# Token forms over all quarters of their stage, S5 parameters in short pieces and S5 two steps later, in a hybrid retention and S5 decoder step on Trainium2

## The chip, the core and the metric

The kernel runs on one core of one Trainium2 chip. The core has five engines that run their own instruction streams and meet at semaphores: TensorE (PE: matmuls, and PEld for its weight loads), VectorE (DVE), ScalarE (ACT), GpSimd (POOL) and SyncE (SP). Transfers are issued by an engine (here SP, ACT and POOL) and carried by 16 DMA engines. The metric is the time of one execution on the device, in microseconds (us); less is better.

## The reference

One step of a decoder layer over 1024 prompt tokens and 8 sample tokens (1032 columns in all), model width 2048, all in fp32. It is cut here to what matters:

```python
h = rmsnorm(x, g_pre)
proj = h @ w_in                                   # 2048 x 10240
q, k, v, za, ub, zb, ga, gb = split(proj)         # 1024 each, ga and gb 2048
ya = retention(rope(q), rope(k), v, s_ret)        # 8 heads, chunks of 128
yb = s5(ub, ...)                                  # 64 groups, 64 complex states each
ya = (ya * silu(za)) @ w_pa
yb = (yb * silu(zb)) @ w_pb
out = (sigmoid(ga) * ya + sigmoid(gb) * yb) @ w_out
return x + rmsnorm(out, g_post), the new states
```

and the parameters of S5, which the kernel computes from the weights before S5 can begin:

```python
dt = exp(log_dt); mag = exp(lam_re * dt)
abar_r, abar_i = mag * cos(lam_im * dt), mag * sin(lam_im * dt)
coef = (abar - 1) / lam                           # complex
bbar = coef * b                                   # and powers of abar for chunks of 128
```

## The kernel before

Every matmul is done in fp32 by a split: a weight quarter (128 x 512) comes on SP's queue, ACT makes its rounded copy `whi` (L193), DVE the remainder `wlo` (helper `tt`, L84), and PE multiplies `whi` with the high and the low part of the activations and `wlo` with the high part (`three`, L200 to L202). PE runs through the program with almost no gaps. All else is fitted beside it by hand: `bg` is a queue of generators, and `slot()` (L164) runs the next piece of the first of them, up to its next `yield`. The instructions of a piece are placed behind those that PE, ACT and DVE have just been given. So the number of pieces and the number of slots decide when a generator ends; `drain()` runs what is left of all of them at once.

The stages that the change touches, in the order of the program:

1. **Start.** The tokens are loaded and split, two of the eight S5 input tiles (`ubp`, pool `ubw`, two buffers) are computed, and the token norm `rstd`. `scale_ub` scales these two tiles by it on DVE.
2. **Forms stage** (L758 to L760). `linear` computes the other S5 inputs, `M_UB + 3` to `M_UB + 7`: four weight quarters each, 36 matmuls a quarter, and a slot after each, so 20 slots. After the fourth quarter `evac_ub` empties the three PSUM banks of the tile into a `ubp` buffer on DVE (five instructions) and POOL writes the buffer to DRAM (`ub_d`). In the slots `build_forms` (L737) runs: eight rounds, each of which loads two rows of 128 features over all tokens (tile `fx`, four buffers, POOL's queue), scales them on DVE (L744), makes four differences and sums (tiles `fo`, five buffers), and writes seven forms `fm_d` on ACT's queue (L751). These are the activations of a Strassen scheme with seven products.
3. **Product loop** (L1209). 70 steps: 35 pairs of output tiles, for the first half of the features (steps 0 to 34) and for the second. A step has seven products of 24 matmuls (`product`, L857), each with its weights made two products ahead (`prep`, `whi` at L838), and a slot behind each. The results of a product leave PSUM on ACT or DVE (`evac_st`: tiles `p`, `u`, `st`); product 3 writes the bank that product 1 used, and so on, so a late `u` on DVE stops PE. POOL writes four results per step to DRAM (`pt_d`).
4. In step 1 the generator `s5_params` (L379) is put into `bg`: small vector work on tiles of 128 x 64 to 128 x 256. Before, it has six pieces. In step 3 what is left of it is drained, its pool is released, and `s5_all` follows, which has one piece for each of 200 slots, and `s5_out` with one more. S5 uses PE, DVE, ACT and POOL between the products.
5. In step 34 (`NP - 1`) S5's pools are released and the pool `stg2` with twelve buffers takes their place. Through it the 28 token forms of the second half are read back (`stage`, L800, POOL's queue) and split (`unstage`: cast on ACT at L245, difference on DVE at L84) into the activation tiles, form by form as the products of step 34 free them. Step 35 begins the second half.

The order of the instructions on each engine is that of the program as a scheduler lays it out: a load of `stg2` can stand ahead of the results of an earlier step.

Of the kernel before, what the change touches and what calls it, by code (L numbers as in the profile page):

```python
# [10 lines left out]
F32 = mybir.dt.float32  # L11
# [10 lines left out]
TOK = SEQ + NB  # L22
KD = D // 128
# [55 lines left out]
def emit(ctx, tc, I, O):  # L79
# [254 lines left out]
    ubw = ubstack.enter_context(tc.tile_pool(name="ubw", bufs=2))  # L334
# [44 lines left out]
    def s5_params():  # L379
# [16 lines left out]
        def fexp(out, x):  # L396
# [8 lines left out]
            V.scalar_tensor_tensor(t, n, -LN2_LO, t, ALU.mult, ALU.add)  # L405
            V.tensor_scalar(p, t, EXP_POLY[0], None, ALU.mult)
            for cc in EXP_POLY[1:] + [1.0]:
                V.scalar_tensor_tensor(p, p, cc, t, ALU.add, ALU.mult)
            V.tensor_scalar(n, n, 127.0, 8388608.0, ALU.add, ALU.mult)
# [4 lines left out]
        fexp(dt, ld)  # L414
# [3 lines left out]
        fexp(mag, lx)  # L418
        yield
# [6 lines left out]
        V.tensor_scalar(ph, ph, MAGIC, None, ALU.subtract)  # L426
        rr = pt("rr", 2 * N)
# [5 lines left out]
        V.tensor_scalar(rr, rr, PI_CLAMP, -PI_CLAMP, ALU.min, ALU.max)  # L433
        sc = pt("sc", 2 * N)
# [15 lines left out]
        V.reciprocal(den, den)  # L450
        mul(cr, nr, lrs)
# [7 lines left out]
        pp["cr"], pp["ci"] = cr, ci  # L459
        AR = s5q.tile([128, 9, S], F32, name="AR")  # L460
# [6 lines left out]
        for d in (1, 2, 4):  # L467
            s_, o_ = slice(1, d + 1), slice(d + 1, 2 * d + 1)
            br = AR[:, d:d + 1, :].broadcast_to([128, d, S])
            bi = AI[:, d:d + 1, :].broadcast_to([128, d, S])  # L470
            mul(AR[:, o_], AR[:, s_], br)
            mul(t1[:, 0:d], AI[:, s_], bi)
            sub(AR[:, o_], AR[:, o_], t1[:, 0:d])
            mul(AI[:, o_], AR[:, s_], bi)
            mul(t1[:, 0:d], AI[:, s_], br)
            add(AI[:, o_], AI[:, o_], t1[:, 0:d])
        pp["AR"], pp["AI"] = AR, AI
        yield
# [12 lines left out]
        for i in range(10):  # L491
# [12 lines left out]
            if i % 4 == 3:  # L504
                yield
# [231 lines left out]
    def build_forms():  # L737
        for i in range(KD // 8 * 4):
            kh, i = divmod(i, 4)
            t = {}  # L740
            for n, k in (("u", 8 * kh + i), ("v", 8 * kh + 4 + i)):
                r = fb.tile([128, TOK], F32, name="fx", bufs=4)
                P.dma_start(r, I["xT"][k])
                V.scalar_tensor_tensor(r, r, gpre[:, k:k + 1], rstd, ALU.mult, ALU.mult)  # L744
                t[n + "1"], t[n + "2"] = r[:, 0:HT], r[:, HT:TOK]
            for n, a, b, op in (("t1", "u1", "u2", ALU.subtract), ("t3", "u2", "v2", ALU.subtract),
# [6 lines left out]
            yield  # L753
# [455 lines left out]
    for s in range(len(steps)):  # L1209
# [7 lines left out]
        if s == 3:  # L1217
# [406 lines left out]
```

## Time and profile before

| | us |
|---|---|
| median of 3 runs | 2696.56 (2695.28 to 2698.29) |
| the profiled execution, its own time | 2691.63 |
| its span in the profile | 2689.8 |
| mean granted clock of PE in it | 0.995 |

The span runs from the first to the last recorded instruction; the profiled execution took 1.8 us more than that. In a timeline a row is: start, busy time, engine, line, operation, output and inputs with their shapes, how many instructions of one kind in a row, and in brackets how long the engine was idle ahead of them and what released it. In a window the row begins with its stretch and length, then the busy time of PE, PEld, DVE, ACT and POOL with the number of instructions, the granted clock of PE (1.00 is full speed), the busy share of the DMA engines and what they moved in GB/s. PE's wide matmuls of the product loop follow one another every 0.12 us, so 24 of them take 2.9 us, and a step of seven products 20.2 us.

### The profile page before, as it was taken

How to read it: one execution, taken by the hardware profiler on the slowest of the kernel's cores; microseconds unless marked ns; L12 is line 12 of the kernel's file. 1: busy time of each engine (PE TensorE's matmuls, PEld its weight loads, DVE VectorE, ACT ScalarE, POOL GpSimd, SP SyncE). 2: the span in 40 equal slices, each digit the busy share in tenths (PEclk: the TensorE clock that was granted, in tenths of full speed). 3: DMA queues.
4: the chain of work that ended last, by engine and by line, in shares of the span. 5: the costliest groups of instructions: out<-in, count | busy, mean ns of one | idle time of the engine just before them, and what ended most of it. 6: DMA issues, size and time to landing. Idle time of an engine off the chain costs nothing.

```text
span 2689.8 us, 50001 instructions
## 1 busy us (share of the span) xinstructions
PE 2640.3 (98%) x19268; PEld 2572.4 (96%) x19268; DVE 1706.6 (63%) x3648; ACT 906.2 (34%) x1607; POOL 743.4 (28%) x1205
## 2 busy tenths in 40 slices
PE   9999999999999999999999999999999999999988
PEld 8999999999999999999999999999999999998866
DVE  6645988988988867558867666665422344335455
ACT  6013232332333335442234444444411122333333
POOL 0103222222222222322244434332032354112020
PEclk9999999999999999999999999999999999999999
DMA  5886444444444457876688778777244444435575
GB/s 186 273 249 195 136 127 124 123 127 132 119 130 127 125 175 215 207 194 158 164 224 231 212 204 215 185 211 241 77 147 141 137 142 142 146 125 184 166 238 167
DMA packets 209615, 458.71 MB, mean 171 GB/s; under 512 B 30832, under 2 KB 51776, under 8 KB 209248
## 3 DMA queue, kind: packets, MB, share of 16 engines
q0 software_dynamic: 87344, 252.19, 33.5%
q1 hardware_dynamic: 102496, 180.63, 22.1%
q10 hardware_dynamic: 19536, 22.69, 2.8%
q8 instruction: 151, 2.47, 0.4%
q14 instruction: 88, 0.72, 0.1%
HBM read 318.12 MB, written 137.27 MB: 169 GB/s over the span
## 4 chain that ended last, share of the span: by engine, by line
PE 85%; DVE 5%; DMA 5%; issue 3%; ACT 2%; POOL 1%; ACTq 0%; DVEq 0%; SPq 0%; POOLq 0%
PE acc L857 46%; PE mm L200 9%; PE mm L201 9%; PE mm L202 9%; PE mm L1524 5%; PE misc L1524 1%; DMA wraw<-in_w_outB 1%; DVE wlo L84 1%; DVE a L84 1%; DMA fm_d<-fo 1%; DVE u L84 1%; PE misc L621 1%; PE misc L699 1%; PE misc L698 1%; PE misc L1064 1%
## 5 line engine op out<-in xcount | busy, mean ns | idle before, releaser
L857 PE MATMUL acc<-a,whi 128*128 128x258 f32 x7840 | 1276.8, 285 | 14.0 <-DVE u L84 7.8
L857 PEld LDWEIGHTS acc<-a,whi 128*128 128x128 f32 x7840 | 1079.8, 190 | 21.4 <-DVE u L84 9.8
L857 PE MATMUL acc<-a,wlo 128*128 128x258 f32 x3920 | 790.1, 283 | 0.0
L84 DVE TENSOR_TENSOR wlo<-wraw,whi 128x512 fp32r<-128x512 f32 x547 | 384.3, 703 | 417.8 <-ACT whi L193 334.9
L857 PEld LDWEIGHTS acc<-a,wlo 128*128 128x128 f32 x3920 | 607.2, 190 | 0.0
L200 PE MATMUL mm<-a,whi 128*128 128x384 f32 (+2 forms) x1584 | 513.3, 325 | 12.2 <-ACT whi L193 7.9
L201 PE MATMUL mm<-a,whi 128*128 128x384 f32 (+2 forms) x1584 | 513.1, 324 | 0.2 <-DVE a L352 0.2
L202 PE MATMUL mm<-a,wlo 128*128 128x384 f32 (+2 forms) x1584 | 511.4, 323 | 0.3
L838 ACT CAST whi<-wraw 128x512 fp32r<-128x512 f32 x280 | 173.7, 620 | 503.1 <-PE acc L857 393.4
L193 ACT CAST whi<-wraw 128x512 fp32r<-128x512 f32 x267 | 165.0, 619 | 521.7 <-PE mm L201 328.7
L200 PEld LDWEIGHTS mm<-a,whi 128*128 128x128 f32 x1584 | 298.4, 189 | 13.4 <-ACT whi L193 8.3
L202 PEld LDWEIGHTS mm<-a,wlo 128*128 128x128 f32 x1584 | 299.9, 189 | 1.6 <-DVE wlo L84 1.5
L201 PEld LDWEIGHTS mm<-a,whi 128*128 128x128 f32 x1584 | 298.7, 189 | 0.6 <-DVE a L352 0.6
L838 ACT CAST whi<-wr 128x512 fp32r<-128x512 f32 x210 | 130.1, 620 | 417.4 <-PE acc L857 390.4
L84 DVE TENSOR_TENSOR wlo<-wr,whi 128x512 fp32r<-128x512 f32 x210 | 143.7, 684 | 42.9 <-ACT whi L838 41.8
L1524 PE MATMUL mm<-whi,a 128*128 128x512 f32 x352 | 121.7, 403 | 4.0 <-ACT whi L193 4.0
L84 DVE TENSOR_TENSOR st<-mm,sz 128x384 f32<-128x384 f32 (+1 forms) x96 | 49.4, 515 | 92.8 <-PE mm L202 53.2
L84 DVE TENSOR_TENSOR wraw<-wr 128x512 f32<-128x512 f32 x140 | 95.9, 685 | 1.7
L911 POOL DMA_DIRECT2D u<-pt_d x70 | 62.0, 886 | 114.1 <-DVE u L84 92.7
L84 DVE TENSOR_TENSOR p<-acc,p 128x516 f32<-128x516 f32 x70 | 48.4, 692 | 67.1 <-PE acc L857 67.0
L909 POOL DMA_DIRECT2D pt_d<-u x70 | 38.7, 553 | 188.5 <-DVE u L84 140.5
L1524 PEld LDWEIGHTS mm<-whi,a 128*128 128x128 f32 x352 | 67.3, 191 | 21.8 <-ACT whi L193 6.2
(358 smaller groups left out, 3244.5 us busy)
## 6 DMA issues: line engine op xcount, KB each, us to landing
wr<-in_w_in SPq DMA_DIRECT2D x280, 256.0 KB
wraw<-in_w_outB SPq DMA_DIRECT2D x102, 256.0 KB
pt_d<-u POOLq DMA_DIRECT2D x70, 258.0 KB, 3.1
u<-pt_d POOLq DMA_DIRECT2D x70, 258.0 KB, 5.3
stg<-fm_d POOLq DMA_DIRECT2D x56, 258.0 KB, 4.7
wraw<-in_w_out SPq DMA_DIRECT2D x53, 256.0 KB
pt_d<-st POOLq DMA_DIRECT2D x35, 258.0 KB, 3.1
pt_d<-p POOLq DMA_DIRECT2D x35, 258.0 KB, 3.0
```

Source lines behind the costliest of these rows:

```text
L84: return (eng or V).tensor_tensor(out, a, b, op)
L193: anchor["a"] = A.copy(hi, raw).ins
L200: T.matmul(ps, wh[:, i, :], xh[:, t0:t1], start=first, stop=False)
L201: T.matmul(ps, wh[:, i, :], xl[:, t0:t1], start=False, stop=False)
L202: anchor["p"] = T.matmul(ps, wl[:, i, :], xh[:, t0:t1], start=False, stop=last).ins
L621: T.matmul(ps[0:16, g * 128:(g + 1) * 128], B1[:, g, :], W3[:, g, 0:8, :], start=True, stop=True)
L698: T.matmul(o, Tm[:, g, :], U[:, g, 0:136], start=True, stop=False)
L838: anchor["a"] = A.copy(hi, f).ins
L857: anchor["p"] = T.matmul(ps[:, j, 0:258], a[:, i, :], b[:, 258 * j:258 * j + 258], start=first and i == 0 and a is wh and b is xh, stop=n ...
L909: P.dma_start(pt, t)
L911: P.dma_start(t, pt, accum_op=ALU.add)
L1524: anchor["p"] = T.matmul(ps[c], a, b, start=k == 0 and a is xh and b is wh, stop=k == KD - 1 and a is xl).ins
```

## The change

It has four parts.

- `build_forms` loads the token rows of a round one round ahead, and its first slot does nothing but load. A round is a piece with the scalings (and the next loads), and a piece with the differences and the writes; every second round has an empty piece behind it. That is 1 + 8 x 2 + 4 = 21 yields instead of 16, so that the work reaches over all 20 slots of the stage.
- The pool `ubw` has three buffers instead of two.
- `s5_params` gives way 22 times instead of 5: 23 pieces for the 28 slots of the steps 1 to 4.
- S5 begins in step 5 instead of step 3. (The short description says pairs: a step works on one pair.) Its 201 slots then reach into step 33, not 31.

The diff, cut to its core:

```diff
-    ubw = ubstack.enter_context(tc.tile_pool(name="ubw", bufs=2))
+    ubw = ubstack.enter_context(tc.tile_pool(name="ubw", bufs=3))
...
+            yield
             V.tensor_scalar(p, t, EXP_POLY[0], None, ALU.mult)
             for cc in EXP_POLY[1:] + [1.0]:
                 V.scalar_tensor_tensor(p, p, cc, t, ALU.add, ALU.mult)
+            yield
             V.tensor_scalar(n, n, 127.0, 8388608.0, ALU.add, ALU.mult)
...
-        fexp(dt, ld)
+        yield from fexp(dt, ld)
...
-        fexp(mag, lx)
-        yield
+        yield from fexp(mag, lx)
...
             mul(t1[:, 0:d], AI[:, s_], br)
             add(AI[:, o_], AI[:, o_], t1[:, 0:d])
+            yield
         pp["AR"], pp["AI"] = AR, AI
-        yield
...
-            if i % 4 == 3:
-                yield
+            yield
...
     def build_forms():
-        for i in range(KD // 8 * 4):
-            kh, i = divmod(i, 4)
+        raw = {}
+
+        def load(j):
+            for n in range(2):
+                k = 8 * (j // 4) + j % 4 + 4 * n
+                raw[k] = fb.tile([128, TOK], F32, name="fx", bufs=4)
+                P.dma_start(raw[k], I["xT"][k])
+
+        load(0)
+        yield
+        for j in range(8):
+            kh, i = divmod(j, 4)
             t = {}
             for n, k in (("u", 8 * kh + i), ("v", 8 * kh + 4 + i)):
-                r = fb.tile([128, TOK], F32, name="fx", bufs=4)
-                P.dma_start(r, I["xT"][k])
+                r = raw.pop(k)
                 V.scalar_tensor_tensor(r, r, gpre[:, k:k + 1], rstd, ALU.mult, ALU.mult)
                 t[n + "1"], t[n + "2"] = r[:, 0:HT], r[:, HT:TOK]
+            if j < 7:
+                load(j + 1)
+            yield
...
             for p, n in enumerate(FORMS):
                 A.dma_start(fm_d[kh, p, i], t[n])
             yield
-            yield
+            if j % 2:
+                yield
...
-        if s == 3:
+        if s == 5:
```

Four more single `yield` lines in `s5_params` are left out. All lines behind the change stand up to 17 further down in the new program, so L744 becomes L757, L800 becomes L817 and L909 becomes L926. How it moves the instructions shows at three places.

**DVE at the start of the forms stage.** `ubp<-ubp` are the scalings of tiles 0 and 1, `ubp<-mm` the emptying of tile 2's banks, `fx` and `fo` the first round of the forms, `wlo<-wx` a weight split. Before:

```order
L84 TENSOR_TENSOR ubp<-ubp,rstd 128x128x8
L84 TENSOR_TENSOR ubp<-ubp,rstd 128x8 x2
L744 SCALAR_TENSOR_TENSOR fx<-fx,g_pre,rstd 128x1032
L84 TENSOR_TENSOR wlo<-wx_841,whi 128x512
L744 SCALAR_TENSOR_TENSOR fx<-fx,g_pre,rstd 128x1032
L84 TENSOR_TENSOR fo<-fx 128x516
L84 TENSOR_TENSOR ubp<-mm,rstd 128x48x8 x2
L84 TENSOR_TENSOR ubp<-mm,rstd 128x32x8
L84 TENSOR_TENSOR ubp<-mm,rstd 128x8 x2
```

and in the changed kernel:

```order
L84 TENSOR_TENSOR ubp<-ubp,rstd 128x128x8
L84 TENSOR_TENSOR ubp<-ubp,rstd 128x8 x2
L84 TENSOR_TENSOR ubp<-mm,rstd 128x48x8 x2
L84 TENSOR_TENSOR ubp<-mm,rstd 128x32x8
L84 TENSOR_TENSOR ubp<-mm,rstd 128x8 x2
L757 SCALAR_TENSOR_TENSOR fx<-fx,g_pre,rstd 128x1032 x2
L84 TENSOR_TENSOR wlo<-wx_841,whi 128x512
L84 TENSOR_TENSOR fo<-fx 128x516 x2
```

The five instructions that empty tile 2's banks now stand ahead of the first scalings of tokens.

**DVE in step 1, between the emptying of product 1's bank and that of product 3's.** Before, the two rows with a tile `u` have 60 rows between them; the last of these, the second `u` itself and what follows it:

```order
L84 TENSOR_TENSOR AR<-AR,pw_2856 128x64
L84 TENSOR_TENSOR ci<-ci,den 128x64
L84 TENSOR_TENSOR AI<-AR,AI 128x64
L84 TENSOR_TENSOR pw_2856<-AI,AR 128x64
L84 TENSOR_TENSOR AR<-AR 128x128
L84 TENSOR_TENSOR AI<-AI,pw_2856 128x64
L84 TENSOR_TENSOR u_2907<-acc,p_2694 128x516
L84 TENSOR_TENSOR pw_2856<-AI 128x128
```

In the changed kernel there are 19 rows between them, and the parameters are still at their second exponential:

```order
L401 TENSOR_SCALAR e_t<-lx 128x96
L402 TENSOR_SCALAR e_n<-e_t 128x96
L403 TENSOR_SCALAR e_n<-e_n 128x96
L404 SCALAR_TENSOR_TENSOR e_t<-e_n,e_t 128x96
L405 SCALAR_TENSOR_TENSOR e_t<-e_n,e_t 128x96
L407 TENSOR_SCALAR e_p<-e_t 128x96
L409 SCALAR_TENSOR_TENSOR e_p<-e_p,e_t 128x96
L84 TENSOR_TENSOR u_2834<-acc,p_2694 128x516
```

Most of the parameters' rows have moved behind later products.

**POOL at the end of S5.** `pt_d` are the four results that each step writes (`st`, `u`, `p`, `u`), `stg<-fm_d` the 28 loads of token forms. Before, from the results of step 31 on:

```order
L909 DMA pt_d<-st 128x516
L800 DMA stg<-fm_d 128x516 x2
L909 DMA pt_d<-u_11994 128x516
L800 DMA stg<-fm_d 128x516 x3
L909 DMA pt_d<-p_11876 128x516
L800 DMA stg<-fm_d 128x516 x2
L909 DMA pt_d<-u_11933 128x516
L800 DMA stg<-fm_d 128x516 x9
L909 DMA pt_d<-st 128x516
```

Then come the remaining results of steps 32 and 33, eight loads, the first result of step 34 and the last four loads. In the changed kernel, from the results of step 33 on:

```order
L926 DMA pt_d<-st 128x516
L817 DMA stg<-fm_d 128x516 x2
L926 DMA pt_d<-u_12454 128x516
L817 DMA stg<-fm_d 128x516 x3
L926 DMA pt_d<-p_12336 128x516
L817 DMA stg<-fm_d 128x516 x2
L926 DMA pt_d<-u_12393 128x516
L817 DMA stg<-fm_d 128x516 x17
L926 DMA pt_d<-st 128x516
L817 DMA stg<-fm_d 128x516 x4
```

The first seven loads have moved from step 31 to step 33, and the nine that stood a step and a half ahead of step 34 stand in it now, with the other twelve.

More of the change, by code (lines that the diff above doesn't have):

```diff
@@ L503, in s5_params @@
             mul(phi[:, i, :], phi[:, i, :], u1)
-            if i % 4 == 3:
-                yield
+            yield
         pp["phr"], pp["phi"] = phr, phi
@@ L737, in build_forms @@
     def build_forms():
-        for i in range(KD // 8 * 4):
-            kh, i = divmod(i, 4)
+        raw = {}
[5 more added lines that the diff above has]
+        load(0)
+        yield
+        for j in range(8):
+            kh, i = divmod(j, 4)
             t = {}
             for n, k in (("u", 8 * kh + i), ("v", 8 * kh + 4 + i)):
-                r = fb.tile([128, TOK], F32, name="fx", bufs=4)
-                P.dma_start(r, I["xT"][k])
+                r = raw.pop(k)
                 V.scalar_tensor_tensor(r, r, gpre[:, k:k + 1], rstd, ALU.mult, ALU.mult)
                 t[n + "1"], t[n + "2"] = r[:, 0:HT], r[:, HT:TOK]
+            if j < 7:
+                load(j + 1)
+            yield
             for n, a, b, op in (("t1", "u1", "u2", ALU.subtract), ("t3", "u2", "v2", ALU.subtract),
@@ L752, in build_forms @@
             yield
-            yield
+            if j % 2:
+                yield
     M_UB, M_ZB, M_GA, M_GB = 32, 40, 48, 64
```

## The prediction

> **What bounds the kernel now.** I read the page first, then the windows, then PE's waits and the timelines round each wait. The page says that PE works almost throughout, and that the chain which ended last is mostly PE:
>
> ```profile
> span 2689.8 us, 50001 instructions
> PE 2640.3 (98%) x19268; PEld 2572.4 (96%) x19268; DVE 1706.6 (63%) x3648; ACT 906.2 (34%) x1607; POOL 743.4 (28%) x1205
> PE 85%; DVE 5%; DMA 5%; issue 3%; ACT 2%; POOL 1%; ACTq 0%; DVEq 0%; SPq 0%; POOLq 0%
> ```
>
> The change removes no matmul, so it can win only where PE stands still or its clock is low. The windows (stretch, length, busy time of PE, PEld, DVE, ACT and POOL, granted clock, DMA share, GB/s) show the stages that it touches:
>
> ```profile
> 82.00:198.00 116.00, 110.71 (x690) 109.45 (x689) 63.37 (x95) 11.32 (x20) 11.89 (x32) 0.99 0.92 290
> 262.00:284.00 22.00, 22.00 (x185) 21.96 (x183) 16.36 (x61) 6.61 (x10) 7.86 (x16) 1.00 0.60 174
> 284.00:294.00 10.00, 6.12 (x34) 5.49 (x33) 10.00 (x52) 0.87 (x2) 3.12 (x7) 0.83 0.30 87
> 345.00:950.00 605.00, 604.63 (x5012) 597.43 (x5011) 534.70 (x1423) 188.49 (x348) 162.19 (x289) 1.00 0.44 125
> 1016.00:1046.00 30.00, 28.06 (x234) 27.85 (x233) 29.47 (x48) 19.82 (x36) 9.67 (x18) 1.00 0.81 264
> ```
>
> They are the forms stage, a full stretch of the product loop, the S5 parameters, S5 itself, and the step after S5. S5 hides completely (604.63 of 605.00), so moving its body costs and gains nothing; only its two ends matter.
>
> **The forms stage: -7.5.** PE's timeline has its first matmul:
>
> ```profile
> 82.23 0.34 PE L200 MATMUL mm<-a,whi 128*128 128x384 f32 x1
> ```
>
> ACT's timeline has two weight casts, which follow PE one quarter apart:
>
> ```profile
> 186.47 0.62 ACT L193 CAST whi<-wraw 128x512 fp32r<-128x512 f32 x1 [5.03 <-PE mm L201]
> 192.12 0.62 ACT L193 CAST whi<-wraw 128x512 fp32r<-128x512 f32 x1 [5.03 <-PE mm L201]
> ```
>
> An undisturbed quarter takes 192.12 - 186.47 = 5.65 us. The twentieth and last should start at 82.23 + 19 x 5.65 = 189.6, and starts here:
>
> ```profile
> 197.70 0.33 PE L200 MATMUL mm<-a,whi 128*128 128x384 f32 x1
> ```
>
> So 8.1 us are lost. PE's own waits in the stage (total, times, longest) give two parts of it:
>
> ```profile
> PE mm L200 <- DVE ubp L84: 2.8, 1, 2.8
> PE mm L200 <- ACT whi L193: 2.3, 1, 2.3
> ```
>
> The windows round the second wait give a third:
>
> ```profile
> 125.00:130.00 5.00, 2.63 (x11) 2.31 (x12) 2.76 (x4) 1.14 (x2) 0.75 (x3) 0.89 1.09 320
> 130.00:135.00 5.00, 5.00 (x28) 5.00 (x27) 4.20 (x6) 0.00 (x0) 0.00 (x0) 0.77 0.99 258
> ```
>
> A quarter is 36 matmuls, 6.4 per us; these ten us hold 39 instead of 64, a loss of 3.9, of which 2.3 is the second wait and 1.6 the low clock after it (0.77). The remaining 1.4 of the 8.1 is scattered.
>
> *First wait.* PE goes on when DVE has emptied a bank of output tile 2:
>
> ```profile
> 89.34 0.36 PE L200 MATMUL mm<-a,whi 128*128 128x264 f32 x1 [2.76 <-DVE ubp L84]
> ```
>
> It wanted the bank at 89.34 - 2.76 = 86.6. DVE's timeline shows why it was late:
>
> ```profile
> 78.74 4.12 DVE L84 TENSOR_TENSOR ubp<-ubp,rstd 128x1024 f32<-128x1024 f32 x6
> 83.84 1.30 DVE L744 SCALAR_TENSOR_TENSOR fx<-fx,g_pre,rstd 128x1032 f32<-128x1032 f32 x1 [0.97 <-DMA fx<-in_xT]
> ...
> 88.39 1.98 DVE L84 TENSOR_TENSOR ubp<-mm,rstd 128x384 f32<-128x384 f32 x5 [0.84 <-DMA ub_d<-ubp]
> ```
>
> The five instructions of the last row wait for a write-back that frees one of two buffers, and stand behind two scalings of 1.3 us. With a third buffer, and with the first slot loading tokens only, they follow the row at 78.74 directly: start 83.84 - 0.97 = 82.9, end 84.9, before 86.6. What is late next is the weight split behind them: two scalings (2.6) and a `wlo` (0.7) end at about 88.2, and PE reaches the quarter that wants it at 82.23 + 5.65 = 87.9. I leave 0.6 standing.
>
> *Second wait.* DVE had waited for a token load:
>
> ```profile
> 120.92 1.29 DVE L744 SCALAR_TENSOR_TENSOR fx<-fx,g_pre,rstd 128x1032 f32<-128x1032 f32 x1 [4.86 <-DMA fx<-in_xT]
> ```
>
> So its form writes came late on ACT's queue, and the weight cast behind them too:
>
> ```profile
> 126.59 1.14 ACT L193 CAST whi<-wx 128x512 fp32r<-128x512 f32 x2 [13.96 <-DMA fm_d<-fx]
> ```
>
> Loads a step ahead take out the 4.86, more than the 2.31 that reached PE. The same 16 loads and 56 writes (two and seven in each of eight rounds) remain, over 20 quarters instead of 16; transfers fill a share of 0.92 of the stage, so they are the cover that could fail. A load still waits on POOL for a buffer that older form writes free; queued behind it there are the clearing and the write-back of the next `ubp`, which the third buffer now gives a whole tile more time. Bounds: -2.8 (only the first wait goes) to -8.1; I take 8.1 - 0.6 = **-7.5**, near the upper, because both releasers in the rows go.
>
> **S5 parameters: -5.5.** The third window holds 34 matmuls in 10 us, where 185 in 22 (8.4 per us) is normal: 34 / 8.4 = 4.0, so 6.0 are lost. PE's timeline has 3.9 of it as waits; the other 2.1 is low clock (0.83):
>
> ```profile
> 285.00 0.75 PE L857 MATMUL acc<-a,whi 128*128 128x258 f32 x4 [0.83 <-ACT whi L838]
> 288.29 0.75 PE L857 MATMUL acc<-a,whi 128*128 128x258 f32 x4 [2.54 <-DVE u L84]
> 293.46 0.74 PE L857 MATMUL acc<-a,whi 128*128 128x258 f32 x4 [0.52 <-DVE u L84]
> ```
>
> DVE's timeline has the rows that empty products 1 and 3 of that step:
>
> ```profile
> 276.98 0.68 DVE L84 TENSOR_TENSOR u<-p,acc 128x516 f32<-128x516 f32 x1
> 287.55 0.69 DVE L84 TENSOR_TENSOR u<-acc,p 128x516 f32<-128x516 f32 x1
> ```
>
> They are 10.57 us apart. The order shows 60 DVE rows between them, 10.57 / 60 = 0.18 us each. With 23 pieces, one per product over 28 slots, 19 rows stand there: 19 x 0.18 = 3.4 us, below the two products that lie between, whose length comes from the chain's row of one seven-product step:
>
> ```profile
> 360.62 20.18 PE acc L857 x168
> ```
>
> Two products are 2 x 20.18 / 7 = 5.77. Nothing else becomes late: steps 1 to 4 have no other background work. Bounds: -4.0 (a piece with a slow function load still makes one wait) to -6.0; I take **-5.5**. At the start of S5 PE waits once, and the pieces there are unchanged:
>
> ```profile
> 331.82 0.36 PE L857 MATMUL acc<-a,whi 128*128 128x258 f32 x1 [1.01 <-DVE a L84]
> ```
>
> Between 0 and -1.0 I take **-0.5**, since another phase of the loop may or may not hide it. Gains: **-13.5**.
>
> **S5 later: +7.9.** S5 needs 201 slots at seven a step: from step 3 it ends in step 31, from step 5 in step 33. Its memory then becomes the `stg` pool, through which 28 token forms are read for the second half; they must be split before step 35 can pass its second product. POOL's timeline shows when it issued them:
>
> ```profile
> 970.00 1.08 POOL L800 DMA_DIRECT2D stg<-fm_d x2 [4.54 <-PE acc L857]
> ...
> 979.79 4.24 POOL L800 DMA_DIRECT2D stg<-fm_d x8
> ```
>
> The view of the tile shows their splits and the time from issue to landing:
>
> ```profile
> L84 DVE TENSOR_TENSOR a<-stg,a x28: 685/687/699, 975.1 to 1037.3; 128x516 fp32r<-128x516 f32 x28
> ...
> DMA to landing us min/median/max: 2.9/5.4/7.2
> ```
>
> PE's timeline shows the wait behind them:
>
> ```profile
> 1040.55 0.62 PE L857 MATMUL acc<-a,whi 128*128 128x258 f32 x3 [1.94 <-ACT whi L838]
> ```
>
> Sixteen loads went out early and twelve in step 34, and the cast behind the last splits already costs PE 1.94. After the change the order puts only 7 ahead of the row that was at 979.79; the other 21 follow from 979.79 + 2 x 20.18 = 1020.2 (times of before). Behind the first, which takes 5.4, come 26 transfers: 20 loads and some six weights and results. The window in which the early loads fell shows what full queues moved:
>
> ```profile
> 986.00:989.00 3.00, 3.00 (x28) 3.00 (x26) 1.99 (x3) 0.62 (x1) 0.09 (x1) 1.00 1.03 400
> ```
>
> At 400 GB/s, 258 KB (264,192 bytes) take p = 0.66 us. The last lands at 1020.2 + 5.4 + 26 x 0.66 = 1042.8. A cast (0.62) and split (0.69) follow, then what lay between the last split's end and PE's return, 1040.55 - (1037.3 + 0.69) = 2.6. PE returns at 1046.7: **+6.1** (in general 26p - 11.05). The idle stretch is then 1.94 + 6.1 = 8.0 us in one piece. In the rows above waits of 2.31 and 2.54 brought the clock down and cost 1.6 and 2.1 more, while 2.76 and 1.94 did not; for one of 8.0 I add their mean, **+1.8**. Bounds of the whole: +2.7 (loads in time, only four more splits of 0.69 on a DVE busy 29.47 of 30) to +17 (p = 1.0, the pace of 264 GB/s in the window of before, with the clock). I take +7.9, by the row of 400 GB/s.
>
> [...]
>
> **Sum.** -13.5 + 7.9 = -5.6. The profiled execution took 2691.63, and would take 2686.0; the median of the three runs is 4.9 above it (2696.56), so the forecast for the median is 2691.0. A measurement of this kernel tells 0.2% (5.4 us) from no change.
>
> **Rivals.**
> - *The end is cheap.* Splits keep up, DVE alone adds 2.7 and no clock is lost: -10.8, 2685.8. For it: POOL issued loads every 0.53 us (eight in 4.24); against it: 21 of them queue at once.
> - *The forms' second wait stays*, since transfers fill 0.92 of the stage: +4.7 on the forecast, -0.9, 2695.7.
> - *Slow loads.* Step 34's splits and weights share the queues, p = 0.9: 26 x 0.9 - 11.05 + 1.8 = 14.2, net +0.7, 2697.3.
> - *The pieces free nothing*: DVE in steps 1 to 4 stays as packed, the parameters' term is 0: -0.1, 2696.5.
> - *Slower: the token forms come at a pace worse than that of before's window.* The price passes the gain by 5.4 where 26p - 11.05 + 1.8 = 18.9, at p = 1.08 (244 GB/s). At p = 1.2 it is +21.9, net +8.4, 2705.0. For it: twelve buffers, each freed only by a split, pace the loads; against it: 264 GB/s were moved with DVE full.
>
> **How the numbers follow.** Forecast 0.48, of which 0.27 lies beyond -5.4 and 0.21 within; cheap end 0.19; second wait stays 0.11; slow loads 0.10; pieces 0.04; slower 0.08. Faster: 0.27 + 0.19 = 0.46. Same: 0.21 + 0.11 + 0.10 + 0.04 = 0.46. Slower 0.08. The range runs from the cheap end less 2.8 (2683.0; the runs of before spread over 3.0) to slow loads plus 2.7 (2700.0); the slower case lies outside. The forecast's own range is 2687 to 2695.
>
> **What would show it.** In the changed profile: no `ubp` wait of PE in the forms stage, and its twentieth quarter 6.5 to 8 us earlier after the first; no wait above 0.8 on `u` in the parameters, the clock there at 1.00; all S5 windows full; and before the second product of step 35 one wait of PE of some 8 us, on a `whi` behind the last splits, with a clock below 1 after it. It is wrong if that wait is about 5 or less (faster than forecast) or above 14, or if a wait of over 2 us on `whi` stands in the forms stage.

## The result, and the profile after

| | us |
|---|---|
| changed kernel, median of 4 runs | 2676.4 (2674.38 to 2680.78) |
| before, beside it, median of 4 runs | 2696.1 (2695.28 to 2698.29) |
| ratio | 0.9927, 95% interval 0.9916 to 0.9939 |
| profiled execution, its own time | 2676.77 |

The change makes the kernel 0.7% faster by this comparison, 19.7 us by the medians. The forecast was 5.6, and 2676.4 lies 6.6 us below the range. Repeated twice on other occasions the changed kernel had ratios of 0.9948 (0.9931 to 0.9965) and 0.9955 (0.9942 to 0.9967); the mean of the three, 0.9943, is 15 us. The intervals of the first and the third comparison do not overlap, so the ratio depends on the occasion by more than one interval tells: at 0.9948 or 0.9955 the time beside 2696.1 would be 2682.1 or 2684.0, at the lower end of the range (2683.0).

The page of the changed kernel has the same matmuls and nearly the same shares, in 14.8 us less:

```profile
span 2675.0 us, 49998 instructions
PE 2634.6 (98%) x19268; PEld 2569.0 (96%) x19268; DVE 1710.2 (64%) x3648; ACT 907.4 (34%) x1607; POOL 742.8 (28%) x1205
```

Its windows over the stretches shown of before (columns as there):

```profile
82.00:198.00 116.00, 116.00 (x739) 116.00 (x738) 66.88 (x102) 13.05 (x21) 12.17 (x31) 1.00 0.97 287
284.00:294.00 10.00, 10.00 (x86) 10.00 (x85) 9.32 (x34) 3.46 (x6) 3.41 (x7) 1.00 0.59 189
345.00:950.00 605.00, 604.63 (x5013) 597.84 (x5012) 538.79 (x1444) 187.64 (x346) 158.28 (x282) 1.00 0.44 124
1016.00:1046.00 30.00, 26.66 (x203) 25.93 (x203) 24.08 (x39) 16.61 (x28) 8.75 (x15) 0.94 0.82 260
```

PE fills the forms stage (116.00 of 116.00) and the time of the parameters (10.00 of 10.00) at full clock, though the transfers of the forms stage still take a share of 0.97. S5's body is hidden as before. At its end PE now loses more: 26.66 busy of 30.00, against 28.06, though the changed kernel is some 8 to 13 us further on in its work there. These are PE's waits from 950 to 1050:

```profile
PE acc L874 <- DVE u L84: 3.0, 2, 2.5
PE acc L874 <- ACT whi L855: 1.9, 1, 1.9
PE acc L874 <- ACT p L964: 1.0, 1, 1.0
PE acc L874 <- ACT a L245: 1.0, 1, 1.0
```

The forecast's price is there, 6.9 us of waits where before had 1.9, but in five pieces spread over steps 34 and 35 instead of one of 8.0. POOL's timeline has the reason that was forecast, the late loads:

```profile
1004.69 4.23 POOL L817 DMA_DIRECT2D stg<-fm_d  x8
...
1020.85 0.54 POOL L817 DMA_DIRECT2D stg<-fm_d  x1 [0.35 <-DVE a L84]
```

Eight loads follow the last result of step 33, and the last of all is issued 16 us later. The view of the tile `stg` has the casts, the last of which starts 21.6 us after the first of these eight loads, and under what its engines sat idle for (us, times), the waits for loads:

```profile
L245 ACT CAST a<-stg x28: 615/623/629, 999.4 to 1026.3; 128x516 fp32r<-128x516 f32 x28
...
  DMA stg<-fm_d: 12.4, 8
```

Before had 7.4. These are splits that stand in the order of ACT and DVE ahead of the emptying of PE's banks and wait for a load.

To compare two kernels step by step I use one mark: the start of ACT's copy that empties product 0 of a step. For step 36, where the second half has begun, before and after:

```profile
1061.36 0.58 ACT L947 COPY p<-acc 128x516 f32<-128x516 f32 x1
```
```profile
1053.02 0.58 ACT L964 COPY p<-acc 128x516 f32<-128x516 f32 x1
```

So 8.3 of the 14.8 us are won up to there. The same marks for the profiles of all kernels, as differences to the first profile of before (us; "half" counts the halved stretches of the clock ahead of the last matmul, which the section on the clock explains; where S5 begins in step 4 or 5, its start lies behind the mark of step 4):

| profile | step 0 | step 2 | step 4 | step 36 | last matmul | span | half |
|---|---|---|---|---|---|---|---|
| before | 0 | 0 | 0 | 0 | 0 | 0 | 4 |
| before, again | -2.7 | -2.9 | -2.6 | -1.1 | +2.0 | +2.0 | 7 |
| changed | -8.4 | -14.6 | -16.0 | -8.3 | -12.1 | -14.8 | 1 |
| changed, again | -8.7 | -14.8 | -16.3 | -9.5 | -12.4 | -15.1 | 2 |
| changed, third | -9.0 | -15.2 | -16.6 | -11.4 | -12.6 | -15.3 | 3 |
| forms only | -8.6 | -8.9 | -8.9 | -8.9 | -10.1 | -10.1 | 2 |
| changed, two `ubp` buffers | -3.7 | -9.9 | -11.3 | -4.4 | -1.8 | -4.6 | 5 |
| pieces only | -2.1 | -8.3 | -9.7 | -4.0 | -1.2 | -0.9 | 4 |
| pieces and S5 in step 5 | -1.1 | -7.3 | -8.7 | -2.6 | -3.8 | -6.0 | 3 |
| S5 in step 5 only | -1.5 | -2.2 | -3.6 | +3.5 | +2.6 | +0.4 | 5 |
| S5 in step 4 only | -2.3 | -2.8 | -4.2 | -2.5 | -1.2 | -4.0 | 6 |
| S5 in step 2 only | -1.5 | -1.9 | +3.3 | +2.4 | +3.1 | +0.3 | 7 |
| changed, S5 in step 3 | -8.4 | -14.6 | -16.0 | -9.6 | -7.1 | -7.0 | 5 |
| the same, 14 pieces | -8.8 | -15.0 | -16.2 | -9.6 | -10.3 | -10.2 | 5 |
| S5 in step 4, 18 pieces | -8.3 | -14.5 | -15.9 | -12.6 | -13.2 | -15.9 | 2 |
| the same, again | -8.6 | -14.8 | -16.2 | -13.0 | -17.1 | -19.8 | 2 |
| the same, splits on POOL | -8.4 | -14.6 | -16.0 | -10.4 | -9.4 | -12.1 | 2 |

### The profile page after: what moved, and what is told of

It is laid out like the page before. It is cut to its first block, busy times and chain, and to the rows that moved or that the text cites. A ratio compares the mean times of both kernels' runs of the same rounds, so it can differ in the third digit from the quotient of the medians.

```text
span 2675.0 us, 49998 instructions
## 1 busy us (share of the span) xinstructions
PE 2634.6 (98%) x19268; PEld 2569.0 (96%) x19268; DVE 1710.2 (64%) x3648; ACT 907.4 (34%) x1607; POOL 742.8 (28%) x1205
## 4 chain that ended last, share of the span: by engine, by line
PE 84%; issue 7%; DVE 3%; DMA 3%; POOL 2%; ACT 1%; DVEq 0%; POOLq 0%; ACTq 0%; SPq 0%
PE acc L874 42%; PE mm L200 10%; PE mm L201 10%; PE mm L202 10%; PE mm L1541 5%; PE misc L1541 2%; DMA wraw<-in_w_outB 1%; DVE wlo L84 1%; DMA xr<-in_xT 1%; DVE a L84 1%; DMA stg<-fm_d 1%; PE misc L625 1%; PE misc L703 1%; PE misc L702 1%; PE misc L1081 1%
## 5 line engine op out<-in xcount | busy, mean ns | idle before, releaser
L926 POOL DMA_DIRECT2D pt_d<-u x70 | 38.6, 552 | 178.4 <-DVE u L84 129.5
```

The source lines that it names most:

```text
L926: P.dma_start(pt, t)
```

## The experiments

### Before and the changed kernel, again

The kernels are unchanged; the question is what differs between two executions of one program.

> The kernel before, unchanged, for a second profile and more times. Known so far: the profiled executions differ by 14.8 us, of which 8.5 stand at the last step of the product loop (step 69) and 6.3 come after it, where the profile of before shows a clock of 0.93 and 0.86 in its last 90 us; the medians differ by 19.7. Theory A (the parts change only the first 1050 us, the rest is the granted clock of the output stage, which varies from execution to execution): time 2690 to 2698, ratio 1.000, step 69 at the same 1827.3 within 1 us, and the stretch from there to the end, 862.5 in the profile of before, differs by 2 us or more in this one. Theory B (the output stage of before is slower for a reason in the program): the stretch is 862.5 again within 1 us.

Measured: 2691.3 (2686.8 to 2695.8, 11 runs), ratio 0.9996 (0.9987 to 1.0005). The second profile of before differs from the first by 2.7 at step 0, by 1.5 between steps 35 and 36, and by 3.3 between steps 36 and 69. Neither theory has it right as written: the stretch behind step 69 is the same (862.3 against 862.5, as B said), but step 69 is not (+2.1). What holds is that stretches with the same instructions take different times, ahead of step 69 too.

> The changed kernel unchanged, for a second profile and more times beside the same runs of before. Found in the six traces so far: the clock is halved in stretches of 3.41 us on a grid whose phase differs from execution to execution, each time after a stretch of that grid in which PE stood idle for 0.51 or more of it, and never after one of 0.50 or less; a halved stretch costs 1.7 us. Theory C: waits of some 2 to 3 us therefore cost 1.7 more in some executions and not in others, and the change removes four such waits and adds others. Counted over all phases of the grid, the trace of before has 6.6 halved stretches on average and that of the changed kernel 3.5, so 5.3 us on top of the 9.0 by which the spans differ without them: 14, ratio 0.995, time 2679. Theory D (first comparison taken as it is, with something in the output stage that is faster for good): ratio 0.9927 again, 2673.5.

Measured: 2676.6 (2675.1 to 2680.4, 5 runs) beside 2693.8, ratio 0.9948. Theory C's count of 14 us agrees (0.52% of 2694 is 14.0, and the interval spans 9 to 19 us); D's 0.9927 lies just outside the interval. But one sentence of C fell: here a stretch with PE idle for 0.44 of it was followed by a halved one.

> The changed kernel unchanged, once more beside the others on one chip. Sum of what was found: about -8 up to step 36, -2.7 behind the last matmul, -2 to -3 in the three places of the second half where waits and halved stretches differ from run to run: -13, ratio 0.995 (0.9927 and 0.9948 so far). Rival: 0.9927 is the true one, -19.

Measured: 2679.5 (2676.3 to 2683.2, 5 runs) beside 2690.6, ratio 0.9955: the sum of -13 is met within the interval, the rival's 0.9927 is not.

### The forms stage: the whole part, and the third buffer

Forms only: the diff's hunks for `build_forms` and `ubw`, nothing else.

> Before with the forms part alone (loads a step ahead, 21 yields, three ubp buffers). By the comparison of the two traces, step 0 of the product loop comes 8.4 us earlier and nothing else moves up to step 69. Theory A: -8.4 up to step 69, and a total of -8.4 give or take 6 for the clock of the output stage: 2682 to 2694, ratio 0.995 to 0.999. Theory B, if the forms part is the cause of the other 11 us: -19, 2677, ratio 0.993.

Measured: 2682.4 (2681.5 to 2687.4, 5 runs), ratio 0.9963 (0.995 to 0.9977). Step 0 comes 8.6 earlier than in the quoted profile of before and nothing moves from there to step 36, as A said. But 0 is the latest of the seven profiles that have the old forms stage: their mean is -1.6, that of the ten with the new one -8.6, so the part is worth 7.0.

```diff
-    ubw = ubstack.enter_context(tc.tile_pool(name="ubw", bufs=3))
+    ubw = ubstack.enter_context(tc.tile_pool(name="ubw", bufs=2))
```

> The changed kernel with two ubp buffers instead of three. In the order the emptying of tile 2's banks stands behind two scalings of tokens again. Theory: the first wait (2.8 on ubp) returns, and with it in most executions a halved stretch (1.7); the second wait (2.3 on whi) stays away: +2.8 to +4.5 at step 0 against the changed kernel, ratio to before 0.0010 to 0.0017 higher than its. Rival: the loads a step ahead take the first wait away too, since they land before DVE needs them: nothing at step 0.

Measured: ratio 0.9972 (0.9961 to 0.9983), 0.0024 above the changed kernel beside it, and step 0 at -3.7, 4.9 later than in the changed kernel; both are a little more than expected. PE's waits in the forms stage of this kernel:

```profile
PE mm L200 <- DVE ubp L84: 3.4, 1, 3.4
```

The first wait is back, so the third buffer is what takes it out. With the 3.4 comes one halved stretch (1.7). The rival falls. That the second wait stays away here says less, for the second profile of the kernel before does not have it either:

```profile
PE mm L200 <- DVE ubp L84: 3.3, 1, 3.3
```

Of the seven profiles with the old forms stage, four have waits on `whi` there (0.6, 1.0, 1.4 and 2.3 us in total) and three have none; of the eleven with the loads a round ahead none has one. So the loads do take this wait out, but the profile that the prediction read had the largest of them. By step 0 the third buffer is worth 4.9 of the 7.0 us, and the rest of the part about 2.1 (from one profile).

### The parameters in pieces

Pieces only: the diff's hunks in `s5_params`.

> Before with the parameters in 23 pieces alone; S5 still begins in step 3, so that only 14 slots run pieces and 9 pieces are drained in one go. In the changed kernel the pieces over 28 slots brought 6.2 us up to step 2. Theory A: the drained pieces hold about two fifths of the rows and cost a wait on u again: -2 to -4 up to step 6, and 2688 to 2697, ratio 0.998 to 1.000. Rival: the drained pieces are only the late ones, which DVE catches up on as the first products of step 3 run: the full -6.2, ratio 0.9975. Theory B, if this part is the cause of the other 11 us: ratio 0.994 or less.

Measured: ratio 0.9996 (0.9988 to 1.0005). Step 2 has the full 6.2, and 4.2 of it are gone at step 5 (-5.5). The expectation put that on the 9 pieces that are drained at once. This was tested with the other parts in place, S5 back in step 3, with 23 and with 14 pieces:

```diff
-        if s == 5:
+        if s == 3:
```

> The changed kernel with S5 back in step 3, so that one part is undone: 14 slots for the 23 pieces, 9 drained at once. By the parts measured so far: -7 at step 0, -6.2 to step 2, then +4.2 where the 9 pieces are drained, no price at the end of S5: some -9 to -10 at step 36 against the mean of before, against -8 for the changed kernel. GpSimd's last drain was 8.8 us in the four kernels with S5 in step 3 and 4.8 to 4.9 in the eight others, with S5 in step 2, 4 or 5: 8.8 here, and the span ends 13.4 after the last matmul, not 10.7, which takes 2.7 back. Together ratio 0.995 to 0.997, above that of the changed kernel in the same call. Rival: the drain was chance or belongs to other parts, 10.7 after the last matmul, and the ratio is at or below that of the changed kernel.

and, beside that line, in `s5_params`:

```diff
             V.scalar_tensor_tensor(t, n, -LN2_LO, t, ALU.mult, ALU.add)
-            yield
...
-            yield
+            if i % 3 == 2:
+                yield
```

> As the last, but with the parameters in 14 pieces, one for each slot of steps 1 and 2 (an exponential gives way once, the last loop every third time). If the 4.2 came from the 9 drained pieces: -6 to step 2, no loss behind it up to step 5, -12 to -14 at step 36. Rival: the heavier pieces make products wait on u again within steps 1 and 2: -3 or less up to step 2.

Measured: ratios 0.9967 (0.9955 to 0.998) and 0.9974 (0.9962 to 0.9985), both above the changed kernel's 0.9955 beside them, as the first expectation had it, though the intervals overlap. Both lose 4.9 and 5.2 between step 4 and step 5 (-16.0 and -16.2 become -11.1 in both), though the second drains nothing; its expectation of -12 to -14 at step 36 missed (-9.6). So it is not the drained pieces. PE's waits from 290 to 360 in the two kernels:

```profile
PE acc L874 <- DVE u L84: 3.0, 1, 3.0
```
```profile
PE acc L874 <- DVE a L605: 2.2, 1, 2.2
PE acc L874 <- DVE p L84: 0.6, 1, 0.6
PE acc L874 <- DVE u L84: 0.2, 1, 0.2
```

Before had 1.5 of waits there. Each of the two has a halved stretch behind its wait besides. What S5's first two steps take beyond 20.17 us each, the length of a step without other work, can be compared in all kernels: 2.7 with S5 in step 5 and in the kernel before with S5 in step 4, 4.1 and 4.4 in the two profiles of before, 6.9 to 8.1 with the longer lists of pieces and S5 in step 3. My reading is that S5's first dense work follows on DVE without a pause when the parameters fill the slots right up to it. It is not shown: the six pieces of before leave eight slots free and still lose 1.4 there. The heavier pieces of the second kernel cost nothing up to step 2 (-6.2 as well), so its rival falls too.

> Before with the parameters in 23 pieces and S5 in step 5, without the forms part. Alone, the pieces had 9 of them drained in step 3 and lost there 4.2 of the 6.2 that they had won. Together: -6.2 at step 2, -1.4 at S5's start, +7.7 at its end, so 0 at step 36 beside its own step 0, and a ratio of 0.999 to 1.001. Rival: the two parts and the forms part gain more together than apart (sum of the three apart: -11.8 us, together -19.7 in the first comparison), and this one has the rest: ratio 0.997.

The kernel is before with the hunks in `s5_params` and with S5 in step 5. Measured: 2686.4 (2682.6 to 2696.7, 12 runs), ratio 0.9981 (0.9967 to 0.9995). The marks go as expected up to the end of S5: -6.2 to step 2, -1.4 to step 4, then +6.1 to step 36. The total is below the expected one, by 5 us, and 2.2 of them lie behind the last matmul, where no theory had looked yet. The rival's 0.997 lies inside the interval too.

### The step in which S5 starts

```diff
-        if s == 3:
+        if s == 5:
```

> Before with S5 in step 5 alone. The comparison of the traces gave +7.7 between the steady part of S5 and step 36, the forecast was +7.9. Theory A: the first 1.0 wait of S5's start may go, the end costs 7.7: +6 to +8 at step 36, 2698 to 2706, ratio 1.001 to 1.004. Rival: the price at the end was paid only since the other parts had moved it to another phase: nothing at step 36, ratio 1.000. Theory B, if starting S5 later is the cause of the other 11 us: ratio 0.997 or less.

Measured: ratio 0.9999 (0.9989 to 1.001). Step 4 to step 36 costs 7.2, as A said, but its total was wrong: nothing of the price is left. The time was won back behind step 36: the stretch from there to the last matmul took 1614.0 (before 1615.0 and 1618.1), and from the last matmul to the span's end 11.3 instead of 13.4.

The second part of that is no accident of one run. DVE's last work and the end of the span, before and after:

```profile
2680.91 2.74 DVE L1498 SCALAR_TENSOR_TENSOR a<-a,small 128x512 f32<-128x512 f32 x4 [0.67 <-POOL small L1493]
```
```profile
2668.85 2.74 DVE L1515 SCALAR_TENSOR_TENSOR a<-a,small 128x512 f32<-128x512 f32 x4 [0.67 <-POOL small L1510]
```

2689.8 - 2683.65 = 6.2 us pass in the one and 2675.0 - 2671.59 = 3.4 in the other. The last line of the program has the drains that every engine does; POOL's row in the view of that line, for before, the changed kernel, S5 back in step 3, and S5 in step 2 (the durations are the least, the median and the longest in ns):

```profile
L1619 POOLq DRAIN  x3: 51/102/8767, 2680.3 to 2689.6; - x3
```
```profile
L1636 POOLq DRAIN  x3: 51/102/4765, 2668.2 to 2674.7; - x3
```
```profile
L1636 POOLq DRAIN  x3: 51/93/8767, 2673.2 to 2682.5; - x3
```
```profile
L1619 POOLq DRAIN  x3: 51/102/4847, 2683.4 to 2689.9; - x3
```

Step 4 and step 2 were tried on the kernel before:

```diff
-        if s == 3:
+        if s == 4:
```

> Before with S5 in step 4, nothing else changed. In the traces so far GpSimd's last drain takes 8.8 us in the four kernels with S5 in step 3, so that the span ends 13.4 to 13.8 after the last matmul, and 4.8 to 4.9 in the six with S5 in step 4 or 5, where it ends 10.7 to 11.3 after it. If that goes with the step in which S5 starts: 10.7 to 11.3 here. If it goes with the other parts (only one kernel of the six has none of them): 13.4. The price at the end of S5: as in the changed kernel with S5 in step 4, +0 to +3 at step 36; ratio 0.998 to 1.000.

```diff
-        if s == 3:
+        if s == 2:
```

> Before with S5 in step 2, a step earlier. If the span's end after the last matmul goes with the start of S5, it is 13.4 to 13.8 here (or more); if a later or earlier start both change the order of DMAs and with it the drain, 10.7. At the end of S5 all 16 early loads go a step earlier, which should bring nothing: the wait of 1.9 ahead of the second product of step 35 belongs to DVE's splits and stays, 1.9 within 0.2.

Measured: S5 in step 4 alone 2687.7 (2685.7 to 2690.8, 11 runs), ratio 0.9988 (0.9979 to 0.9996), with a price of 1.7 from step 4 to step 36 and a span end 10.7 after the last matmul; S5 in step 2 alone (one run) 2691.9, and also 10.7, against the first reading. Its wait ahead of step 35's second product is 1.9, as expected. Counted over all 18 profiles, POOL's last drain takes 8.8 us in the six with S5 in step 3 and 4.8 to 4.9 in the twelve with S5 in step 2, 4 or 5, whatever the other parts. So it goes with step 3 itself, not with a late start. The drain is 4.0 shorter and the end only 2.7 earlier, because SP's waits on the same line end last then: in the changed kernel POOL's drain ends at 2668.2 + 4.8 = 2673.0 and SP's first drain there starts at 2674.2; in before these are 2689.1 and 2686.2. Why POOL drains longer with S5 in step 3 is not shown.

Between step 5 and step 3 lies step 4. With 18 pieces the parameters fit into the 21 slots of steps 1 to 3:

```diff
-            yield
+            if i % 2:
+                yield
...
-        if s == 5:
+        if s == 4:
```

> The changed kernel with S5 in step 4, and the parameters in 18 pieces (their last loop gives way every second time), so that they fit into the 21 slots of the steps 1 to 3. The order then has 16 loads of token forms ahead of step 34 again, not 7. If the price at the end of S5 comes from those 7: the 7.7 us between the steady part of S5 and step 36 fall to 0 to 2, the gains at step 0 (8.4) and step 2 (6.2) stay, and the time is 5 to 8 us below the changed kernel, ratio to before 0.991 to 0.993. Rival: the price comes from DVE, which must do four more splits beside a full step; it stays at 5 or more, ratio 0.994 to 0.996.

> The kernel with S5 in step 4 and 18 pieces, again, beside the changed kernel on one chip: 3 us below it (12.6 against 9.5 at step 36), ratio 0.0010 to 0.0014 lower. Rival: what is saved at the end of S5 is lost to halved stretches later; equal.

Measured: ratios 0.9934 (0.9916 to 0.9952) and 0.9933 (0.9921 to 0.9946), beside the changed kernel's 0.9948 and 0.9955 on the same chips; medians 2674.7 against 2676.6 and 2673.1 against 2679.5. Step 4 to step 36 costs 3.3 and 3.2, where the changed kernel pays 5.2 to 7.7. But 1.9 and 1.6 of that lie in step 4 itself, where S5 begins three slots behind the last of the pieces. In this kernel PE waits there, from 290 to 360:

```profile
PE acc L875 <- DVE u L84: 1.5, 1, 1.5
```

What is left for the end, 1.5, is what the second profile of before has too. So the first expectation was right about the end (0 to 2): with 16 loads ahead of step 34 the price is gone. Its total was too good, 0.0014 (some 4 us) below the changed kernel instead of 5 to 8 us, since the start of S5 costs something again. The second comparison has 0.0022 (some 6 us), more than the 0.0010 to 0.0014 expected. The intervals overlap each time, but both ratios are lower, so this version is the best that was found. PE's only wait left at the end of S5:

```profile
PE acc L875 <- ACT whi L856: 1.9, 1, 1.9
```

It is the wait that before has, behind DVE's 24 splits of step 34. I tried to take work off DVE there:

```diff
-        split(qslot(kh, n, i), stq.pop((kh, n, i)))
+        hi, lo = qslot(kh, n, i)
+        src = stq.pop((kh, n, i))
+        A.copy(hi, src)
+        sub(lo, src, hi.bitcast(F32), P if kh and i == 1 and 0 < n < 6 else V)
```

> The kernel with S5 in step 4 and 18 pieces, and five of the 24 splits of step 34 with their difference on POOL instead of DVE (one of four for the forms 1 to 5). If DVE's queue of splits holds up step 35: DVE is free of 5 x 0.69 = 3.4 us there, the wait of 1.9 ahead of product 1 of step 35 goes, and with it the halved stretch that follows it in some executions: 2 to 3.5 us less at step 36, ratio to before 0.992 to 0.9935. Rival: POOL's differences (about 1.4 each) stand between its loads and delay them, and the wait grows to 3 or more.

Measured: ratio 0.9956 (0.9942 to 0.9969), worse than the 0.9934 and 0.9933 of the two other occasions, and step 36 comes 2.2 to 2.6 later than there. The wait of 1.9 is gone and others of 4.4 stand in its place:

```profile
PE acc L878 <- DVE u L84: 4.1, 3, 2.0
PE acc L878 <- DVE wlo L84: 0.3, 1, 0.3
```

The rival was right that it costs more, but not by late loads: in this profile the engines of `stg` sit idle for a load for 0.6 us only. DVE's instructions `u` are late, and DVE's rows show what holds it back: the four of them that run beside POOL's five differences take 1.8 to 2.8 us instead of 0.68. One of them, and POOL's row beside it:

```profile
1013.53 2.19 DVE L84 TENSOR_TENSOR wlo<-wr,whi 128x512 fp32r<-128x512 f32 x1
```
```profile
1013.85 1.32 POOL L84 TENSOR_TENSOR a<-stg,a 128x516 fp32r<-128x516 f32 x1
```

Together the four take 6.1 us longer (8.8 instead of 4 x 0.68), more than the 3.4 that were taken off DVE. Why DVE is slower beside POOL no run here shows.

### The clock: waits of chosen length

```diff
+            for _ in range(LADDER.get(s, 0)):
+                add(cur["u2"], cur["p1"], cur["p1"])
             sub(two(cur["u2"]), two(cur["p1"]), ps)
```

> The changed kernel with extra DVE additions of 128 x 516 (0.69 each; they write a tile that the next instruction overwrites) ahead of the emptying of product 1's bank, in steps 37, 39, 41, 43, 45, 47 and 49, where PE has no other wait: 8, 9, 10, 11, 12, 9 and 10 of them. Two products (5.77) hide some 6.4 of them, so PE should wait about 1.1, 1.8, 2.5, 3.2, 3.9, 1.8 and 2.5 us ahead of product 3. Theory C, corrected (a stretch of 3.41 us of a grid in which PE is idle for about half or more is followed by a halved one; in the ten traces so far always from 0.57 and never below 0.44): no halved stretch after the wait of 1.1, one after each wait above 3, some after those of 1.8 and 2.5, and each of them delays the step by 1.7 beyond the wait. Rival (the clock falls only once a wait has lasted a whole stretch): halved stretches only after the 3.9.

Measured (one run): waits of 1.9, 3.1, 3.8, 6.5, 7.7, 4.1 and 5.3 us (longer than planned, and in each step one of 0.3 to 0.5 on `whi` besides) in the order of the steps, followed by 0, 2, 1, 2, 3, 2 and 2 halved stretches. Beyond all its waits the step took 0.5 more without one, 1.8 with one and 2.2 to 3.0 with two or three. Windows on the grid round the first and the third wait:

```profile
1078.65:1082.06 3.41, 2.41 (x21) 2.20 (x19) 3.34 (x6) 1.63 (x3) 1.46 (x2) 1.00 0.54 157
1082.06:1085.47 3.41, 2.54 (x21) 2.54 (x22) 1.41 (x3) 0.40 (x1) 0.42 (x1) 1.00 0.78 152
1085.47:1088.88 3.41, 2.94 (x24) 2.73 (x24) 1.90 (x3) 1.66 (x2) 0.72 (x2) 1.00 0.31 109
...
1167.38:1170.79 3.41, 3.41 (x30) 3.35 (x28) 3.38 (x6) 1.70 (x4) 1.44 (x2) 1.00 0.37 124
1170.79:1174.21 3.42, 0.15 (x2) 0.00 (x0) 3.35 (x7) 1.56 (x2) 0.00 (x0) 0.99 0.92 210
1174.21:1177.62 3.41, 2.87 (x13) 2.87 (x14) 0.48 (x1) 0.00 (x0) 0.00 (x0) 0.51 0.27 87
1177.62:1181.03 3.41, 2.94 (x25) 2.73 (x24) 1.85 (x3) 1.65 (x2) 0.00 (x0) 1.00 0.00 0
```

The wait of 1.9 falls across a border of the grid; PE is busy for 2.41 and 2.54 of the two stretches, and the clock stays. The wait of 3.8 empties one stretch (0.15 busy), and the next runs at 0.51. The wait of 3.1 is shorter than a stretch and was followed by a halved one too, so the rival falls.

## Why the prediction was wrong

**What bounds the kernel: right.** PE stayed full, and all differences came from where it stood still or ran slowly.

**The forms stage: the sum right, its parts not.** Forecast -7.5, measured -7.0 by the means (-8.4 against the quoted profile, which was the slowest of its kind in this stage). No wait of PE is left there, and full transfers (a share of 0.97) did not keep the second. That the sum fits so well is partly luck: the first wait was put at 2.8, and the third buffer brought 4.9; the loads were put at the other 4.7, and brought about 2.1. Nor did the loads a round ahead end DVE's waits for tokens, as the prediction had it; in the changed kernel DVE still waits longer than the 4.86 of before, only PE no longer feels it:

```profile
140.61 1.29 DVE L757 SCALAR_TENSOR_TENSOR fx<-fx,g_pre,rstd 128x1032 f32<-128x1032 f32 x1 [5.17 <-DMA fx<-in_xT]
```

**S5 parameters: right.** Forecast -5.5, measured 6.2 from step 0 to step 2, less the 0.4 that kernels without the pieces show there: 5.8. **S5's start:** -0.5 forecast, with 1.0 as the bound, -1.4 measured: S5's first two steps take 2.7 instead of 4.1 beyond their 20.17 each. With S5 back in step 3 behind the 23 pieces they take 7.6, so the later start is what keeps the pieces from costing there what they won.

**S5's end: the loads right, the wait and the clock wrong.** Forecast +7.9, measured +7.7, +6.8 and +5.2 from step 4 to step 36 in three profiles, where before has 0 and +1.5; by the means 6.57 - 0.75 = 5.8. The late loads were the cause. From S5's 29th step to step 35 the steps take 9.2 to 11.6 us beyond 20.17 each in the seven profiles whose order has 7 loads ahead of step 34, and 3.9 to 5.6 in the ten with 16 (the kernel with splits on POOL left out). The pace was nearly right too: the last cast starts 21.6 us after the first of the late loads, and the prediction's sum lets the last load land after 5.4 + 26 x 0.66 = 22.6. But it let PE wait once, for 8.0 ahead of the second product of step 35, and that wait is 1.9 as before; one of 5 or less was its own sign of being wrong. PE loses the time in step 34 already, because the emptying of its banks stands behind the waiting splits. And the +1.8 for the clock took the wait of 1.94 in before as one that costs no clock. In the second profile of before the same wait of 1.9 is followed by a halved stretch, and each of the three of the changed kernel has one such stretch in steps 34 and 35, so little of the 1.8 is new.

**The sum: the step that failed.** Up to step 36 the terms come to -7.0 - 5.8 - 1.4 + 5.8 = -8.4 (three profiles of the changed kernel against two of before: -9.2), against -5.6 forecast: 2.1 of the difference is the end of S5 and 0.9 its start. That alone lies inside the forecast's own range. But the prediction then set this sum against one execution of the whole kernel and put everything behind step 36 at nothing, without a reason. It was not nothing: by the same means the stretch from step 36 to the last matmul took 4.2 less and that behind the last matmul 2.7 less, 16.1 together.

- The 2.7 are POOL's last drain, which the prediction never looked at. It is caused by taking S5 out of step 3: undoing that one part brings back the 13.5 from the last matmul to the end, where the changed kernel has 10.7.
- The 4.2 are waits and halved stretches of the same instructions in the second half, most of them at three places (about 1350 to 1520, 1800 and 2600; at all others together the profiles differ by up to 1.0). The stretch took 1611.0 to 1618.1 in 17 profiles (the ladder, which adds waits there, left out): 1611.3 in the one without a halved stretch in it and 1614.3 to 1618.1 in the five with three. How much of it the change brings, and how much is chance in which executions were profiled, stays open: the six profiles with S5 in step 3 have 1613.8 to 1618.1, the eleven others 1611.0 to 1617.5. The ratios, 0.9927 to 0.9955, speak for 12 to 20 us in all; the parts that are shown make 8.4 and 2.7.

The profile of before had a row that could have warned of this, and it was not consulted. Two windows of its end:

```profile
2600.00:2650.00 50.00, 45.84 (x182) 35.43 (x182) 24.44 (x38) 21.48 (x39) 3.72 (x7) 0.93 0.69 213
```
```profile
2676.00:2690.00 14.00, 0.76 (x4) 0.27 (x2) 6.30 (x12) 0.69 (x2) 1.11 (x2) 0.60 0.40 150
```

The 0.93 are two halved stretches, which one profile of the changed kernel (the third) has there too and the first has not. The 0.60 costs nothing, for PE has next to no work left there. A clock below 1 at a place that the change does not touch, in a kernel whose single runs spread from 2683.5 to 2698.8, belongs into the range. It was made of the four terms alone.

**The rivals.** The second wait did not stay, the loads were not slower than taken, and the pieces did free DVE. The slower case did not come: it needed the last load to land 5.4 + 26 x 1.08 = 33.5 us after the first, and 21.6 were enough. The cheap end did not come either: 5.8 lies nearer to 7.9 than to its 2.7. None of the rivals had a gain outside the places that the change touches.

## What to carry to other kernels

Work moved out of one place is paid or won at the two ends of the stage, not in its body: between its first two steps and its last ones S5 took the same time within 0.3 us in all 18 profiles. One step later it cost 1.5 to 1.7 at its end, about what the second profile of before shows without any change (1.5), and two steps later 5 to 8, by the loads that its end releases; at its start it gained about 5 once it no longer ran into the parameters. Before a sum of a few us is set against one profile, a second profile of the same kernel tells which of its rows repeat. And a wait that hardly shows can cost more than its length when it leaves PE idle for 0.56 or more of a stretch of the clock's grid: on the ladder the step with the wait of 1.9 had no halved stretch and took 0.5 beyond its waits, that with 3.8 had one and took 1.8. By these two rows two short waits far apart would be cheaper than one of their sum; that is an estimate, which no run tried.

## What the runs showed of the hardware that was not expected

The granted clock of PE is halved in whole stretches of 3.41 us: in the profile of before it is 0.50 from 128.93 to 132.34 and from 289.35 to 292.76, and 1.00 in the stretches on both sides of each. They lie on one grid per execution (these two begin 47 stretches apart), whose phase differs between executions of the same program: the wait of 1.9 ahead of step 35's second product is followed by a halved stretch in the second profile of before and not in the first (1.00 from 1036 to 1046). Over the records of all 18 profiles, a stretch at full clock in which PE was idle for 0.56 or more was always followed by a halved one (47 times), and one with 0.43 or less never; in between both occur. A halved stretch loses half of its 3.41 if PE is busy all through it, so at most 1.7; on the ladder the step with one took 1.8 beyond its waits and the step without 0.5, a difference of 1.3. The prediction was wrong to tell waits that cost clock from others by their length alone: where the grid lies decides as well. The wait of 2.31 in before leaves PE busy for 1.56 of one stretch, and the next runs at 0.50; the longer one of 2.76 lies across a border, PE is busy for 2.01 and 2.04 of the two stretches, and the clock stays at 1.00.

POOL's drain on the last line takes 8.8 us or 4.8 to 4.9 us, depending on the step in which S5 began over 2,300 us earlier, and the longer one puts off the end of the span by 2.7 us.

In the kernel with splits on POOL, DVE's instructions beside POOL's differences took 1.8 to 2.8 us instead of 0.68, so work moved from DVE to POOL was not work saved on DVE.
